# Residual adds and one weight remainder moved from VectorE to accumulating DMAs, two more block pairs, and modulation work placed elsewhere, in a two-layer hybrid DiT kernel

## The chip, the cores and the metric

The kernel runs on one core of a Trainium2 chip. The metric is the device time of one execution in microseconds (us), and the median over runs counts. TensorE is PE below, VectorE DVE, ScalarE ACT, GpSimd POOL; SyncE (SP) issues the loads.

## The reference, cut to what matters

A batch of one holds 256 latent tokens and 256 context tokens of width 1024, so 512 columns run through layer 0. Layer 0 mixes by a short convolution, layer 1 by attention; the context is dropped inside layer 1.

```python
mod  = (silu(c) @ mod_w[i] + mod_b[i]).reshape(bsz, 3, 3, 1, D_MODEL)   # shift, scale, gate of 3 branches
lat  = lat + 0.5 * mod[:, 0, 2] * _swiglu(_modulate(lat, norm_g[i, 0], mod[:, 0, 0], mod[:, 0, 1]), w13, w2)
h    = _modulate(lat, norm_g[i, 1], mod[:, 1, 0], mod[:, 1, 1])          # rms norm, scale, shift
lat  = lat + mod[:, 1, 2] * mixer(h)                                     # conv (layer 0), attention (layer 1)
lat  = lat + 0.5 * mod[:, 2, 2] * _swiglu(_modulate(lat, norm_g[i, 2], ...), w13, w2)
# the context goes through the same lines with modc, until attention has read it
def _swiglu(h, w13, w2):
    gte, up = jnp.split(h @ w13, 2, axis=-1)
    return (jax.nn.silu(gte) * up) @ w2
```

All data is float32.

## The kernel before

**Split products.** Every float32 operand of a product is split into a high part (`hi`, rounded to the PE's float32r by an ACT copy) and a low part (`lo = src - hi`, a DVE subtract); `split` (L107) does both. A product is three matmuls: hi*hi, hi*lo, lo*hi (`mm3`, L127). Weights are loaded by SP into `wr` (8 buffers of 128x1024), and split into `wh`, `wl` (4 buffers of each).

**Tokens lie along the free axis.** The residual stream `x` is 128 x 8 x 512: 8 tiles of 128 channels, 256 latent and 256 context columns. Stream `s` 0 is the latent, 1 the context. Four stages run over both streams: the first feed-forward block ("ffn(0,0)", L1060), the convolution (L1063) with its output product, ffn(0,1) and ffn(1,0). Attention and the last feed-forward block run over the latent alone.

**A feed-forward block** (`ffn`, L754) goes in three parts of 8, 7 and 7 hidden tiles ("thirds"). Of each hidden tile, gate and up are either computed as they are (`w13_mm`: 48 matmuls of 512 columns), or by `Pair` (L675), a block scheme that needs seven products of half blocks in place of eight (84 matmuls of 256 columns). `AS_IS` (L25) lists the tiles of the first third that are computed as they are. A pair needs sums of activation blocks (`sums`, tiles `T1` to `T4`) and of weight blocks (`sums`, L696: three DVE instructions on the raw weights, and splits); its block A22 is split into `w4h`, `w4l` (two buffers of each, L709) and used last, in `four`.

**The second product** (`project`, L569) turns the hidden tiles of a third into 8 output tiles, m = 0 to 7: two or three first ones together, then one by one. `finish` (L547) adds each to the residual: for both streams one DVE instruction `x = py * gate + x` that reads PSUM (L553). In the last third, and in the convolution's output product, a `tail` follows each output tile: `square_add` (L247) squares the tile on ACT and adds to `acc` on DVE. There the last two tiles, m = 6 and 7, are made separately for each stream, first the latent, so that the latent's norm (`rms_sum`: sum over channels by PE on `acc` and the last square, tile `ss`) can run under the context's matmuls. Norm, shift and splits of the next input follow. The places where such a tail runs: end of ffn(0,0), convolution's output product, end of ffn(0,1), end of ffn(1,0).

**Modulation.** The vectors `mod` of both layers are computed on DVE in 224 units in all, each a multiply-reduce over 128x1024 (`mod_unit`, L167, tile `junk`), with weights loaded by SP through the same `wr` buffers (from `in_modT`), two units or four to a 1024-wide load pair. They are strewn over the program: `tick(n)` (L210) adds to a debt and emits units. Where a consumer is reached (`mod_ready`, L217), what is missing is emitted at once. A gate is taken as a whole at the first `finish` of a block (`lazy_gate`), and halved for the feed-forward blocks by a DVE instruction (L239).

**Order.** The start (up to L1044) and the attention's heads have an order written out by hand; elsewhere a scheduler orders the instructions of each engine, and each engine then runs in order. Buffers: `gm` and `sg` (3 of each, 128x512) hold intermediate products and squares; PSUM has 6 tiles for products.

Of the kernel before, what the change touches and what calls it, by code (L numbers as in the profile page):

```python
# [9 lines left out]
F32 = mybir.dt.float32  # L10
# [11 lines left out]
NM = 22  # L22
THIRDS = (8, 7, 7)

AS_IS = {(0, 0): range(3, 8), (0, 1): (), (1, 0): ()}  # L25

EARLY = 4
HEADS = 8
# [19 lines left out]
def hybrid_kernel(ctx: ExitStack, tc: tile.TileContext, a: dict, out: bass.AP):  # L48
# [13 lines left out]
    def nm(s):  # L62
        uid[0] += 1
        return f"{s}{uid[0]}"
# [102 lines left out]
    def mod_unit(l, ch, pair, raw, j, v):  # L167

        mt = mod_tile(l, ch)
        kt = pair * 2 + j  # L170
        col = ch * KT + kt
        junk = mp.tile([P, D], BF16, name=nm("junk"), tag="junk", bufs=1)
        nc.vector.tensor_tensor_reduce(  # L173
            out=junk,
            in0=raw[j],
            in1=scbc[:, v, :],
            scale=1.0,
            scalar=modb[:, l, col : col + 1],
            op0=ALU.mult,
            op1=ALU.add,  # L180
            accum_out=mt[:, kt, v : v + 1],
        )
        done[l, ch] += 1

    def streams(l, ch):
        return 1 if l == 1 and ch >= 5 else 2
# [23 lines left out]
    def tick(n):  # L210

        owed[0] += n
        while (jobs or units) and owed[0] >= 1:
            owed[0] -= 1
            next_unit()

    def mod_ready(l, ch):  # L217
        while not ((l, ch) in done and done[l, ch] == 8 * streams(l, ch)):
            next_unit()
        return modv[l, ch]  # L220
# [10 lines left out]
        return t  # L231

    def gate_of(l, j):
        m = mod_ready(l, 3 * j + 2)
        if j == 1:
            return m
        t = const.tile([P, KT, 2], F32, name=f"G{l}{j}", tag=f"G{l}{j}")
        nv = 1 if (l, j) == (1, 2) else 2
        nc.vector.tensor_scalar(  # L239
            out=t[:, :, :nv], in0=m[:, :, :nv], scalar1=0.5, scalar2=None, op0=ALU.mult  # L240
        )
        return t


    accs = {}
# [299 lines left out]
        return tail  # L545

    def finish(m, ps, c0, c1, gate, tail, wide=False):  # L547
        g = gate()
        for s in range(2):
            for o in [s * S - c0] if not wide else range(0, T2 if s == 0 else 0, S):  # L550
                if not c0 <= s * S < c1:
                    continue
                nc.vector.scalar_tensor_tensor(  # L553
                    out=x[:, m, s * S : s * S + S],
                    in0=ps[:, o : o + S],
                    scalar=g[:, m, s : s + 1],
                    in1=x[:, m, s * S : s * S + S],
                    op0=ALU.mult,
                    op1=ALU.add,
                )  # L560
        if tail:
            tail(m, c0, c1)
# [6 lines left out]
    def project(ws, src, nk, gate, tail, tot, late, ev, between=()):  # L569

        def products(ps, w, ks, c0, c1, wide=True):
            ms = [src(k, c0, c1) for k in ks]
            if wide and len(ms[0]) == 3:
                return mm_wide(ps, [w(k) for k in ks], ms, ks[0] == 0, ks[-1] == nk - 1)
            for k, m in zip(ks, ms):  # L580
                mm3(ps[:, : c1 - c0], w(k), m[:2], k == 0, k == nk - 1)

        nf = 3 if between else 2
        ahead = {}

        def get(m):
            for i in range(m, min(m + 3, KT)):
                if i not in ahead:
                    ahead[i] = ws(i)
            return ahead[m]  # L590

        w2 = [get(m) for m in range(nf)]
        p2 = [psum("py") for _ in range(nf)]
        cut = nk - 2 if between else nk - 1
        for i in range(nf):
            products(p2[i], w2[i], range(cut), 0, tot)
            if i < len(between):
                between[i]()
        if between:
            for i in range(nf):  # L600
                products(p2[i], w2[i], (nk - 2,), 0, tot)
        for i in range(nf):
            products(p2[i], w2[i], (nk - 1,), 0, tot)
            finish(i, p2[i], 0, tot, gate, tail, len(src(0, 0, tot)) == 3)
            tick(ev)

        for m in range(nf, KT - late):
            if tail and tot == S and m == KT - 2:
                ready()
            w = get(m)  # L610
            ps = psum("py")
            wide = len(src(0, 0, tot)) == 3 and m < KT - 1
            products(ps, w, range(nk), 0, tot, wide)
            finish(m, ps, 0, tot, gate, tail, wide)
            tick(ev)
        if late:

            wl = [get(m) for m in (6, 7)]
            if tail:
                ready()  # L620
            for s in range(2):
# [53 lines left out]
    class Pair:  # L675
# [4 lines left out]


        def __init__(self, src, h):
            self.h, self.w = h, {}
# [12 lines left out]
        def sums(self, n):  # L696

            r1, r2 = self.raw
            s1, s2 = r1[:, :T2], r1[:, T2:]
            tt = nc.vector.tensor_tensor  # L700
            if n == 0:
                tt(out=s1, in0=s1, in1=r2[:, :T2], op=ALU.subtract)
                tt(out=s2, in0=s2, in1=s1, op=ALU.subtract)
                self.keep(("S1", "S2"), r1)
                return
            self.w["A22"] = [
                wp.tile([P, T2], F32R, name=nm(t), tag=t, bufs=2) for t in ("w4h", "w4l")
            ]
            split(*self.w["A22"], r2[:, :T2])  # L709
            v = lambda t: t.rearrange("p (a c) -> p a c", a=2)  # L710
            tt(  # L711
                out=v(r2), in0=v(r2), in1=s2.unsqueeze(1).to_broadcast([P, 2, T2]),
                op=ALU.subtract,
            )
            self.keep(("S3", "S4"), r2)
# [38 lines left out]
    def ffn(l, b, h, tot, gate, tail, gs=(), ev=1.5, z=None):  # L754
        gs = list(gs)
        i0 = 0
        for t, n in enumerate(THIRDS):
            between = ()
            if tot == T2:
# [22 lines left out]
                for i in range(len(gs), n):  # L782
                    if t == 0 and not heads and i in AS_IS[l, b]:
# [12 lines left out]
                        w13_mm(pp, w, h, range(4, KT), 0, T2)  # L796
                        gs.append(new_pair("g"))
                        w13_post(pp, gs[-1], 0, T2)
                        tick(4)
                        continue  # L800
                    if heads:
                        pr = heads.pop(0)
# [44 lines left out]
            def ws2(m):  # L847
# [13 lines left out]
                gate, tail if end else None, tot, 2 if end and tot == T2 else 0, ev, between,  # L861
            )
            gs = []

    def lazy_gate(l, j):
        box = []

        def get():
            if not box:
                box.append(gate_of(l, j))  # L870
            return box[0]

        return get


    h = Plain()
# [170 lines left out]
    for i in range(3):  # L1047
        gs0.append(new_pair("g"))
        w13_post(pps[i], gs0[i], 0, T2)

    with tc.issue_after(rows["last"]):
        convk = cload("convk", [P, 3, KT])
        qg = cload("qg", [P, 1])
        kg = cload("kg", [P, 1])
        cosT = cload("cosT", [P, S])
        sinT = cload("sinT", [P, S])


    hn = Plain()
    ffn(0, 0, h, T2, lazy_gate(0, 0), tail_norm(0, 1, hn), gs0, 2)  # L1060
    h = hn

    zs = []  # L1063
    for m in range(KT):
# [4 lines left out]
        for c0, c1 in ((0, S), (S, T2)) if m == 0 else ((0, T2),):  # L1069
# [14 lines left out]
        nc.vector.tensor_scalar(  # L1084
            out=d, in0=u, scalar1=convk[:, 1, m : m + 1], scalar2=None, op0=ALU.mult
        )
# [11 lines left out]
        nc.vector.tensor_tensor(out=z, in0=d, in1=pb, op=ALU.mult)  # L1098
        zs.append(new_pair("z"))
        split(zs[m][0], zs[m][1], z)  # L1100
        tick(5)

    def by_pairs(key, box=None):
        box = box or {}
# [235 lines left out]
    with tc.manual_schedule(engines={e.engine for e in (nc.tensor, nc.vector, nc.scalar, nc.gpsimd)}):  # L1340
# [29 lines left out]
    hn, hz = Beside(), Early()  # L1370
    roomy.append(True)
    project(
        by_pairs("wo", wos), lambda k, c0, c1: aos[k], KT, lazy_gate(1, 1), tail_early(1, 2, hn, hz), S, 0, 0,
    )
    ffn(
        1, 1, hn, S, lazy_gate(1, 2),
        lambda m, c0, c1: nc.sync.dma_start(out[m], x[:, m, :S]), z=hz,
    )

# [79 lines left out]
```

## Time and profile before

| what | value |
|---|---|
| runs of before | 1571.21, 1571.43 and 1567.75 us; median 1571.21 |
| profiled execution | 1571.47 us; its span from first to last instruction 1569.7 us, so 1.8 us lie around it |
| busy share: PE, DVE, ACT, POOL | 99%, 85%, 47%, 2% |
| mean granted TensorE clock | 0.998 |

A profile is read here in this order: the page's busy shares; the chain of work that ended last; then the waits of the engine that the chain names, in the stretch that a change touches. PE's durations overlap, since matmuls are pipelined: one of 512 columns is shown as 389 ns though the next one starts 227 ns later, so the pitch of starts counts, not the duration. "DMA issues" give the time from issue to landing.

### The profile page before, as it was taken

Reading aid. Unit: us, or ns where it says so; the run is one execution under the profiler, and the core shown is the slowest. Engines: PE = TensorE matmul, PEld = TensorE weight load, DVE = VectorE, ACT = ScalarE, POOL = GpSimd, SP = SyncE. Lnnn points to the kernel's source line nnn. Section 1 sums busy time; section 2 is a strip of 40 time slices with the busy share of each in tenths; the row PEclk is TensorE's granted clock in tenths of the full one; section 3 lists DMA queues with packets and bytes.
Section 4 is the critical chain, followed back from the end, with each engine's and each line's share of the span. In section 5 each row is a group of like instructions: output and inputs, shape, how many; then the busy total and the mean of one; then the engine's idle time right before and its main releaser. Section 6 shows DMA issues by size and latency. Waiting matters only on the chain.

```text
span 1569.7 us, 25671 instructions
## 1 busy us (share of the span) xinstructions
PE 1557.7 (99%) x10210; PEld 1422.0 (91%) x10210; DVE 1333.4 (85%) x2129; ACT 733.8 (47%) x1213; POOL 25.4 (2%) x20
## 2 busy tenths in 40 slices
PE   9999999999999999999999999999999999999999
PEld 7888998999888899989899899999899889898888
DVE  5998789899997698978989989969978887887676
ACT  5622452545322365435345465435345445674553
POOL 0000000000000000000000000000000002300000
PEclk9999999999999999999999999999999999999999
DMA  9675246355565323542533614533733853366562
GB/s 373 224 237 180 89 132 187 107 173 159 194 209 166 114 75 108 177 146 87 189 126 117 196 41 135 187 108 118 239 112 114 265 154 106 123 207 221 171 199 75
DMA packets 72120, 248.80 MB, mean 159 GB/s; under 512 B 9024, under 2 KB 10816, under 8 KB 72000
## 3 DMA queue, kind: packets, MB, share of 16 engines
q1 hardware_dynamic: 69408, 245.40, 48.0%
q10 hardware_dynamic: 2592, 1.76, 0.4%
q8 instruction: 80, 1.31, 0.3%
q14 instruction: 40, 0.33, 0.1%
HBM read 244.77 MB, written 1.05 MB: 157 GB/s over the span
## 4 chain that ended last, share of the span: by engine, by line
PE 88%; DVE 6%; DMA 2%; ACT 2%; issue 1%; POOL 0%; POOLq 0%; SPq 0%; ACTq 0%; DVEq 0%
PE py L131 8%; PE py L132 8%; PE py L133 8%; PE p L131 6%; PE p L133 6%; PE p L132 6%; PE q L133 5%; PE q L131 4%; PE q L132 4%; PE py L139 2%; PE pu L139 2%; PE pg L139 2%; PE pg L132 1%; PE pg L133 1%; DMA wr<-in_w 1%; PE pu L132 1%
## 5 line engine op out<-in xcount | busy, mean ns | idle before, releaser
L108 ACT ACTIVATE wh<-wr 128x1024 fp32r<-128x1024 f32 (+2 forms) x442 | 393.7, 916 | 361.9 <-PE py L132 119.6
L109 DVE TENSOR_TENSOR wl<-wr,wh 128x1024 fp32r<-128x1024 f32 (+2 forms) x442 | 454.5, 1048 | 95.1 <-ACT wh L108 76.2
L173 DVE CUSTOM_DVE_ANT_0 junk<-wr,scbc,modb 128x1024 bf16<-128x1024 f32 x218 | 279.4, 1282 | 15.2 <-DMA wr<-in_modT 13.1
L131 PE MATMUL py<-gh,wh 128*128 128x512 f32 (+1 forms) x570 | 214.7, 377 | 0.0
L132 PE MATMUL py<-gl,wh 128*128 128x512 f32 (+1 forms) x570 | 214.0, 375 | 0.0
L133 PE MATMUL py<-gh,wl 128*128 128x512 f32 (+1 forms) x570 | 213.9, 375 | 0.0
L133 PEld LDWEIGHTS py<-gh,wl 128*128 128x128 f32 x570 | 108.3, 190 | 19.0
L131 PEld LDWEIGHTS py<-gh,wh 128*128 128x128 f32 x570 | 108.5, 190 | 18.4
L132 PEld LDWEIGHTS py<-gl,wh 128*128 128x128 f32 x570 | 108.5, 190 | 18.2
L131 PE MATMUL p<-th,wh 128*128 128x256 f32 x432 | 122.3, 283 | 0.0
L132 PE MATMUL p<-tl,wh 128*128 128x256 f32 x432 | 122.3, 283 | 0.0
L133 PE MATMUL p<-th,wl 128*128 128x256 f32 x432 | 122.2, 283 | 0.0
L553 DVE SCALAR_TENSOR_TENSOR x<-py,G,x 128x256 f32<-128x256 f32 x189 | 83.5, 479 | 36.3 <-PE py L133 25.1
L133 PE MATMUL q<-bh,wl 128*128 128x256 f32 x320 | 91.5, 286 | 0.1
L131 PE MATMUL q<-bh,wh 128*128 128x256 f32 x320 | 90.9, 284 | 0.4 <-ACT wh L108 0.4
L132 PE MATMUL q<-bl,wh 128*128 128x256 f32 x320 | 90.5, 283 | 0.0
L132 PEld LDWEIGHTS p<-tl,wh 128*128 128x128 f32 x432 | 82.8, 192 | 0.3
L131 PEld LDWEIGHTS p<-th,wh 128*128 128x128 f32 x432 | 82.8, 192 | 0.3
L133 PEld LDWEIGHTS p<-th,wl 128*128 128x128 f32 x432 | 82.8, 192 | 0.0
L108 ACT ACTIVATE w4h<-wr 128x512 fp32r<-128x512 f32 x54 | 33.8, 625 | 75.1 <-DMA wr<-in_w 56.9
L108 ACT ACTIVATE gh<-gm 128x512 fp32r<-128x512 f32 x66 | 41.6, 630 | 56.0 <-DVE gm L751 53.8
L711 DVE TENSOR_TENSOR wr<-wr,wr 128x1024 f32<-128x1024 f32 x54 | 66.0, 1222 | 0.7
(303 smaller groups left out, 3946.3 us busy)
## 6 DMA issues: line engine op xcount, KB each, us to landing
wr<-in_w SPq DMA_DIRECT2D x176, 512.0 KB, 4.5
wr<-in_modT SPq DMA_DIRECT2D x122, 512.0 KB, 4.5
wr<-in_w2b SPq DMA_DIRECT2D x64, 448.0 KB, 3.9
wr<-in_w2a SPq DMA_DIRECT2D x32, 512.0 KB, 4.7
pm<-in_mod SPq DMA_DIRECT2D x16, 512.0 KB, 10.2
wr<-in_cw_cx SPq DMA_DIRECT2D x16, 512.0 KB, 4.7
wr<-in_cw_b SPq DMA_DIRECT2D x8, 512.0 KB, 4.4
wr<-in_cw_out SPq DMA_DIRECT2D x8, 512.0 KB, 3.9
```

Source lines behind the costliest of these rows:

```text
L108: nc.scalar.activation(out=hi, in_=src, func=AF.Copy)
L109: return nc.vector.tensor_tensor(out=lo, in0=src, in1=hi.bitcast(F32), op=ALU.subtract)
L131: nc.tensor.matmul(ps, wh, mh, start=first, stop=False, **kw)
L132: nc.tensor.matmul(ps, wh, ml, start=False, stop=False, **kw)
L133: nc.tensor.matmul(ps, wl, mh, start=False, stop=last, **kw)
L139: nc.tensor.matmul(ps, w[0], m[2], start=first and n == 0, stop=False)
L173: nc.vector.tensor_tensor_reduce(out=junk, in0=raw[j], in1=scbc[:, v, :], scale=1.0, scalar=modb[:, l, col : col + 1], op0=ALU.mult, op1=A ...
L553: nc.vector.scalar_tensor_tensor(out=x[:, m, s * S : s * S + S], in0=ps[:, o : o + S], scalar=g[:, m, s : s + 1], in1=x[:, m, s * S : s * ...
L711: tt(out=v(r2), in0=v(r2), in1=s2.unsqueeze(1).to_broadcast([P, 2, T2]), op=ALU.subtract,)
```

## The change

- `finish`: for both streams together (columns 0 to 511), and outside a tail or for m below 4 in a tail, ACT writes `gy = py * gate` (two instructions of 256 columns) to a `gm` or `sg` buffer, and a POOL DMA adds `gy` to `x`. In a tail the square of these tiles then waits for that DMA. The other tiles stay with DVE.
- `Pair.sums`: ACT writes `w4h`, then `w4l = -w4h`; a POOL DMA adds the raw block from HBM to `w4l`. The DVE subtract goes.
- `AS_IS` of ffn(0,0) shrinks from tiles 3 to 7 to tiles 3 to 5: tiles 6 and 7 become pairs.
- The factor 0.5 goes into the modulation units (and two small DVE instructions halve the bias); a gate is waited for two tiles at a time.
- `project` emits no modulation after m = 5 where two late tiles follow, and none after m = 6 and 7 elsewhere; the other counts rise (for example from 1.5 to 2.6 and 1.6 in ffn(1,0)). In `w13`'s as-is tiles 3 in place of 4 units, in the convolution 4 in place of 5.
- One multiply in the convolution (`d`) moves from DVE to ACT.

```diff
-AS_IS = {(0, 0): range(3, 8), (0, 1): (), (1, 0): ()}
+AS_IS = {(0, 0): range(3, 6), (0, 1): (), (1, 0): ()}
...
-            scale=1.0,
+            scale=0.5 if ch in (2, 8) else 1.0,
...
     def gate_of(l, j):
...
+        ch = 3 * j + 2
+        def get(m):
+            while done.get((l, ch), 0) < (m // 2 + 1) * 2 * streams(l, ch):
+                next_unit()
+            return modv[l, ch]
+        return get
...
     def finish(m, ps, c0, c1, gate, tail, wide=False):
-        g = gate()
+        g = gate(m)
+        if c1 - c0 == T2 and (not tail or m < 4):
+            t = tp.tile([P, T2], F32, name=nm("gy"), tag="sg" if m % 2 else "gm", bufs=3)
+            for s in range(2):
+                d = slice(s * S, s * S + S)
+                nc.scalar.activation(
+                    out=t[:, d], in_=ps[:, d], func=AF.Copy, scale=g[:, m, s : s + 1]
+                )
+            nc.gpsimd.dma_start(out=x[:, m, :], in_=t, accum_op=ALU.add)
+            if tail:
+                tail(m, c0, c1)
+            return
...
             finish(m, ps, 0, tot, gate, tail, wide)
-            tick(ev)
+            if m < (5 if late else 6):
+                tick(ev)
...
-            split(*self.w["A22"], r2[:, :T2])
+            w4h, w4l = self.w["A22"]
+            nc.scalar.activation(out=w4h, in_=r2[:, :T2], func=AF.Copy)
+            nc.scalar.activation(out=w4l, in_=w4h.bitcast(F32), func=AF.Copy, scale=-1.0)
+            nc.gpsimd.dma_start(out=w4l, in_=self.src[:, 1024 : 1024 + T2], accum_op=ALU.add)
...
-                        tick(4)
+                        tick(3)
...
+    for ch in (2, 8):
+        b = modb[:, :, ch * KT : ch * KT + KT]
+        nc.vector.tensor_scalar(out=b, in0=b, scalar1=0.5, scalar2=None, op0=ALU.mult)
...
-    ffn(0, 0, h, T2, lazy_gate(0, 0), tail_norm(0, 1, hn), gs0, 2)
+    ffn(0, 0, h, T2, gate_of(0, 0), tail_norm(0, 1, hn), gs0, (3, 3))
...
-        nc.vector.tensor_scalar(
-            out=d, in0=u, scalar1=convk[:, 1, m : m + 1], scalar2=None, op0=ALU.mult
-        )
+        nc.scalar.activation(out=d, in_=u, func=AF.Copy, scale=convk[:, 1, m : m + 1])
...
-        tick(5)
+        tick(4)
...
-        lazy_gate(0, 1), tail_norm(0, 2, hn), T2, 2, 1.5,
+        gate_of(0, 1), tail_norm(0, 2, hn), T2, 2, 2,
...
-    ffn(0, 1, h, T2, lazy_gate(0, 2), tail_norm(1, 0, hn), (), 1.7)
+    ffn(0, 1, h, T2, gate_of(0, 2), tail_norm(1, 0, hn), (), (2.8, 2.4))
...
-    ffn(1, 0, h, T2, lazy_gate(1, 0), tail_norm(1, 1, hn), (), 1.5)
+    ffn(1, 0, h, T2, gate_of(1, 0), tail_norm(1, 1, hn), (), (2.6, 1.6))
```

More of the change, by code (lines that the diff above doesn't have):

```diff
@@ L233, in gate_of @@
     def gate_of(l, j):
[L234 to L238, printed above, removed]
-        nc.vector.tensor_scalar(
-            out=t[:, :, :nv], in0=m[:, :, :nv], scalar1=0.5, scalar2=None, op0=ALU.mult
-        )
-        return t
+        ch = 3 * j + 2
[4 more added lines that the diff above has]
+        return get
     accs = {}
@@ L682, in __init__ @@
         def __init__(self, src, h):
-            self.h, self.w = h, {}
+            self.h, self.w, self.src = h, {}, src
             self.raw = [load_raw(src[:, c : c + 1024]) for c in (0, 1024)]
@@ L752, in four, with ffn @@
             split(g[0], g[1], self.gm)
-    def ffn(l, b, h, tot, gate, tail, gs=(), ev=1.5, z=None):
+    def ffn(l, b, h, tot, gate, tail, gs=(), ev=(0, 0), z=None):
         gs = list(gs)
@@ L860, in ffn @@
                 else lambda k, c0, c1: (cur[k][0][:, c0:c1], cur[k][1][:, c0:c1]), n,
-                gate, tail if end else None, tot, 2 if end and tot == T2 else 0, ev, between,
+                gate, tail if end else None, tot, 2 if end and tot == T2 else 0, ev[end], between,
             )
             gs = []
[L865 to L873, printed above, removed]
     h = Plain()
@@ L1083, in hybrid_kernel @@
         d = tp.tile([P, T2], F32, name=nm("d"), tag="gm", bufs=3)
-        nc.vector.tensor_scalar(
-            out=d, in0=u, scalar1=convk[:, 1, m : m + 1], scalar2=None, op0=ALU.mult
-        )
+        nc.scalar.activation(out=d, in_=u, func=AF.Copy, scale=convk[:, 1, m : m + 1])
         u2 = u.rearrange("p (s t) -> p s t", s=2)
@@ L1372, in hybrid_kernel @@
     project(
-        by_pairs("wo", wos), lambda k, c0, c1: aos[k], KT, lazy_gate(1, 1), tail_early(1, 2, hn, hz), S, 0, 0,
+        by_pairs("wo", wos), lambda k, c0, c1: aos[k], KT, gate_of(1, 1), tail_early(1, 2, hn, hz), S, 0, 0,
     )
     ffn(
-        1, 1, hn, S, lazy_gate(1, 2),
+        1, 1, hn, S, gate_of(1, 2),
         lambda m, c0, c1: nc.sync.dma_start(out[m], x[:, m, :S]), z=hz,
```

## Prediction

> **What bounds the kernel now.** The page first.
>
> ```profile
> span 1569.7 us, 25671 instructions
> ...
> PE 1557.7 (99%) x10210; PEld 1422.0 (91%) x10210; DVE 1333.4 (85%) x2129; ACT 733.8 (47%) x1213; POOL 25.4 (2%) x20
> ...
> PE 88%; DVE 6%; DMA 2%; ACT 2%; issue 1%; POOL 0%; POOLq 0%; SPq 0%; ACTq 0%; DVEq 0%
> ```
>
> PE is busy 99%, and the chain of waits is PE for 88%. So taking work from DVE shortens nothing by itself; it counts only where PE waits for DVE. The waits of PE between 45 and 1300 us, where all edits lie:
>
> ```profile
> PE ss L268 <- DVE acc L259: 1.5, 1, 1.5
> PE pg L132 <- DVE bl L109: 1.3, 2, 1.0
> PE pq L131 <- ACT hh L305: 0.4, 1, 0.4
> PE q L131 <- ACT wh L108: 0.4, 1, 0.4
> PE pq L132 <- DVE hl L306: 0.3, 1, 0.3
> ```
>
> The longest is the norm at the end of ffn(1,0). Its timeline (start, duration, engine, instruction):
>
> ```profile
> 1248.92 1.28 DVE L173 CUSTOM_DVE_ANT_0 junk<-wr,scbc,modb 128x1024 bf16<-128x1024 f32 x1
> 1250.24 1.28 DVE L173 CUSTOM_DVE_ANT_0 junk<-wr,scbc,modb 128x1024 bf16<-128x1024 f32 x1
> 1251.45 0.88 DVE L553 SCALAR_TENSOR_TENSOR x<-py,G,x 128x256 f32<-128x256 f32 x2
> 1252.24 1.22 DVE L109 TENSOR_TENSOR wl<-wr,wh 128x1024 fp32r<-128x1024 f32 x1
> 1253.37 0.76 DVE L259 TENSOR_TENSOR acc<-acc,sq 128x256 f32<-128x256 f32 x2
> 1254.04 0.48 DVE L553 SCALAR_TENSOR_TENSOR x<-py,G,x 128x256 f32<-128x256 f32 x1
> 1256.91 1.28 DVE L173 CUSTOM_DVE_ANT_0 junk<-wr,scbc,modb 128x1024 bf16<-128x1024 f32 x1 [2.39 <-DMA wr<-in_modT]
> 1258.13 0.42 DVE L259 TENSOR_TENSOR acc<-acc,sq 128x256 f32<-128x256 f32 x1
> ...
> 1251.56 2.25 SPq L104 DMA_DIRECT2D wr<-in_modT  x2
> ...
> 1256.80 0.28 PE L133 MATMUL py<-gh,wl 128*128 128x256 f32 x1
> 1258.60 0.38 PE L268 MATMUL ss<-ones,acc 128*128 128x1 f32 x2 [1.52 <-DVE acc L259]
> ```
>
> DVE stands behind a modulation unit whose weights were issued at 1251.56 and used at 1256.91, and `acc` behind that. PE loses 1258.60 - 1256.80 less a pitch of 0.12 = 1.68 us. The windows over the stall and after it show a second loss (PE, PEld, DVE, ACT, POOL busy; PEclk; DMA share; GB/s):
>
> ```profile
> 1252.00:1259.00 7.00, 5.47 (x46) 5.27 (x45) 4.61 (x10) 2.54 (x4) 0.00 (x0) 1.00 0.62 218
> 1259.60:1266.40 6.80, 6.80 (x34) 6.80 (x33) 4.31 (x13) 2.93 (x6) 0.00 (x0) 0.50 0.50 146
> ...
> 575.63 0.39 PE L132 MATMUL pg<-bl,wh 128*128 128x256 f32 x1 [1.01 <-DVE bl L109]
> ```
>
> For 6.8 us the granted clock is 0.50: half of it, 3.4 us, is lost. Over the span this is 3.4/1569.7 = 0.2%, just what a mean clock of 0.998 lacks. The 1.0 us wait at 575.63 brought no such stretch (the mean leaves room for one). So a stall of 1.7 us cost 5.1 us, one of 1.0 us only itself.
>
> **The change part by part.**
>
> ```profile
> 646.54 0.39 PE L131 MATMUL py<-gh,wh 128*128 128x512 f32 x1
> ...
> 648.80 0.39 PE L132 MATMUL py<-gl,wh 128*128 128x512 f32 x1
> ...
> 649.37 0.28 PE L132 MATMUL p<-tl,wh 128*128 128x256 f32 x1
> ...
> 650.57 0.28 PE L133 MATMUL p<-th,wl 128*128 128x256 f32 x1
> ```
>
> Two more pairs. Ten pitches lie between the first two rows, 0.226 us each, ten between the last two, 0.120 each. Two as-is tiles are 2 x 48 x 0.226 = 21.7 us, two pairs 2 x 84 x 0.120 = 20.2: -1.5 us. A pair costs DVE more, about 3.3 us by the rows below (1024 columns 1222 ns, 512 columns 687 ns; a net 2 x 1024 and 2 x 512 more, less A22), while the as-is tiles' units fall from 20 to 9 (11 x 1.36 = 15 us less). The cover is that room; without it the pairs' splits would be late.
>
> ```profile
> L553 DVE SCALAR_TENSOR_TENSOR x<-py,G,x 128x256 f32<-128x256 f32 x189 | 83.5, 479 | 36.3 <-PE py L133 25.1
> L711 DVE TENSOR_TENSOR wr<-wr,wr 128x1024 f32<-128x1024 f32 x54 | 66.0, 1222 | 0.7
> ...
> L109 DVE TENSOR_TENSOR w4l<-wr,w4h 128x512 fp32r<-128x512 f32 x54 | 37.1, 687 | 1.2 <-ACT w4h L108 1.0
> L257 DVE COPY acc<-sq 128x256 f32<-128x256 f32 x11 | 2.7, 286 | 0.0
> ...
> L108 ACT ACTIVATE w4h<-wr 128x512 fp32r<-128x512 f32 x54 | 33.8, 625 | 75.1 <-DMA wr<-in_w 56.9
> L734 ACT COPY gm<-q 128x256 f32<-128x256 f32 x54 | 19.7, 365 | 41.2 <-PE q L133 41.2
> ...
> POOL pn L1297 <- DVE r L1294: 1323.8, 4, 1320.7
> ```
>
> Residuals by DMA: 64 tiles (3 x 20, and 4 in the convolution's output product) take 128 x 479 ns = 61 us off DVE and put 128 x 365 = 47 on ACT. A22: 54 subtracts, 37 us, off DVE; 56 more copies of 625 ns, 35 us, on ACT. POOL gets 120 DMAs; it has nothing else to do until 1320 us (last row). ACT stays near 52% and hides its part. What DVE's room is worth is only PE's waits for splits at the pairs' starts; the largest, with two more at the queries' start:
>
> ```profile
> 943.29 0.39 PE L131 MATMUL q<-bh,wh 128*128 128x256 f32 x1 [0.39 <-ACT wh L108]
> ...
> 1270.90 0.38 PE L131 MATMUL pq<-hh,wh 128*128 128x256 f32 x1 [0.43 <-ACT hh L305]
> 1271.54 0.39 PE L132 MATMUL pq<-hl,wh 128*128 128x256 f32 x1 [0.26 <-DVE hl L306]
> ```
>
> In pitches (a wait shows as idle only beyond the overlap) the splits' waits add up to 2.8 us; bounds 0 and 2.8, I take half, -1.4. For the queries the built order of after lets two query products take turns over each arriving `hh`, `hl`, where before one ran alone: bounds 0 and 1.5, taken -1.1. The `bl` wait hangs on the norm after PE's own sum and stays. Gates by pairs of tiles, the halving and `d` on ACT: nothing, beside DVE's room; if that were gone, under 1 us.
>
> Modulation off the last tiles. In after one unit, not two, stands ahead of m = 5 in ffn(1,0), so the load at 1251.56 starts 1.3 us earlier. The unit then ends 1.4 us earlier, and 1.68 shrinks to about 0.3, too short for the half clock: -1.4 - 3.4 = -4.8. Bounds: 0 (the load comes as late as before) and -5.1.
>
> The new wait. In a tail the squares of m = 0 to 3 wait for the adds, in ACT's order: adds 0 and 1, squares 0 and 1, gates of m = 2 and 3, squares 2 and 3. Behind them on DVE wait `acc` and all it does for m = 4 and 5. Call the landing L. In ffn(1,0)'s times: m = 5 ends at 1250.8, each of m = 2 to 5 takes 21 x 0.226 = 4.8 us, so m = 1 ends at 1235.8; its gate copy ends at 1236.9, square 1 at 1237.5 + L, the copies of m = 2 and 3 at 1239.1 + L, square 3 at 1239.7 + 2L, `acc` at 1240.5 + 2L. After it DVE has for m = 4: 0.88 + 1.22 + 0.76 + one unit 1.36; for m = 5: 0.88 + 1.22 + 0.76; then `x` 0.4, unit 1.36, `x` 0.4 and the last square 0.4: 9.6 to 10.0 us until the sum, wanted at 1256.9. So DVE must begin by 1246.9: L up to 3.2 us is free, and each us beyond costs 2. By the built orders the tails of ffn(0,1) and the convolution have no units there (free to 4.2), and ffn(0,0) has its sum nine matmuls later (free to 3.7).
>
> ```profile
> wr<-in_w SPq DMA_DIRECT2D x176, 512.0 KB, 4.5
> ...
> wr<-in_w2b SPq DMA_DIRECT2D x64, 448.0 KB, 3.9
> ...
> rt<-kn ACTq DMA_DIRECT2D x16, 64.0 KB, 2.7
> out_lat<-x SPq DMA_DIRECT2D x8, 128.0 KB, 1.7
> ```
>
> No row has an accumulating or a POOL-issued DMA. An add moves 256 KB and touches it twice, so the rows bound L by 1.7 (half the bytes, quiet) and 4.5 (twice the bytes, among other loads). I take 3.1, the middle: no cost. For small new waits I add 0.8, an estimate of half the remaining splits' waits. [...] `w4l` has two buffers and is used a pair later, some 10 us (84 x 0.120): any L in the bounds is hidden.
>
> Sum, against the profiled 1571.5: -1.5 - 1.4 - 1.1 - 4.8 + 0.8 = -8.0: 1563.5. The median shown is 0.3 lower, so the same within a rounding.
>
> **The rivals.** Late adds (slower). At L = 4.8 the four tails cost 2 x (1.6 + 1.1 + 0.6 + 0.6) = 7.8, and those over 1.5 us, two, bring a half clock each: 6.8. 1563.5 + 14.6 = 1578. It decides from about L = 4.7 (beyond 0.3% of 1571, 4.7 us, which a measurement of this kernel can tell from no change). For it: the tail's DMA share of 0.62 above. Against: the 448 KB row lands in 3.9 in such stretches.
>
> The late load stays: the adds share the DMA engines with `in_modT`, and the unit holds up the sum as before. Then -4.8 falls away: 1568.3, within the bound.
>
> POOL held off. Each add is preceded by POOL's work on it; if DVE's instructions shut POOL out while they run, L grows by a unit's 1.3 us to 4.4: tails 2 x (1.2 + 0.7 + 0.2 + 0.2) = 4.6 and two half clocks 6.8, 1575. [...]
>
> **How the numbers follow.** Forecast 0.58, its own range 1560 to 1567 (all gains full: -1.5 - 2.8 - 1.5 - 5.1 = 1560.6); of it 0.54 are faster by over 0.3% and 0.04 not. Late adds 0.26, all slower. Late load 0.09, same. POOL held off 0.07: 0.04 same, 0.03 slower. Faster 0.54, same 0.17, slower 0.29. The range 1560 to 1579 holds the first, third and fourth and half of the late adds.
>
> **What would show it.** Right: mean clock 1.000 before the end of ffn(1,0) and no 0.50 window there; `x <- gy` landing in 2 to 4 us; no wait of `ss` over 1 us; 84 matmuls of 256 in place of 48 of 512 for two tiles; POOL idle in between. Wrong: ACT's `sq` waiting for the adds over 4 us and DVE's `acc` behind it, new half-clock windows at the four tails, `junk` still waiting for `in_modT` at the last sum, or PE waiting for `w4l`.

## The result and the profile after

The changed kernel takes 1660.34 us (median of 4 runs, 1653.94 to 1663.69), the kernel before 1571.32: ratio 1.0565, interval 1.0527 to 1.0604. It is 89 us slower where 8 us less were forecast, and far outside the range. The profiled execution is the fastest of the four, 1653.94 us. From the page of the changed kernel (the line PEclk is the granted clock in 40 slices, in tenths; q0 is the queue of the DMAs that POOL issues, with packets, MB and share of 16 engines' span; the last rows are DMA issues, KB each, us to landing):

```profile
span 1652.1 us, 26266 instructions
...
PE 1577.1 (95%) x10282; PEld 1443.2 (87%) x10282; DVE 1262.2 (76%) x1951; ACT 820.4 (50%) x1417; POOL 130.5 (8%) x140
...
PEclk9999999997999989999999989999989989999999
...
q1 hardware_dynamic: 69408, 245.40, 45.1%
q0 software_dynamic: 17280, 31.46, 11.1%
...
wr<-in_w SPq DMA_DIRECT2D x176, 512.0 KB, 4.8
...
x<-gy POOLq DMA_DIRECT2D x64, 256.0 KB, 6.9
w4l<-in_w POOLq DMA_DIRECT2D x56, 256.0 KB, 5.9
```

DVE did get its room: 85% became 76%. But PE fell from 99% to 95%, and the clock from 0.998 to 0.975. The adds land after 6.9 us, where the forecast took 3.1 and bounded it by 4.5. Where PE waits, in the view of its waits (us in total, times, longest):

```profile
PE q L131 <- ACT gm L751: 30.3, 7, 8.0
PE ss L268 <- DVE acc L259: 28.1, 5, 10.6
PE ss L268 <- ACT sq L251: 5.0, 3, 4.4
```

Two places, then. `ss` is the norm at the end of a tail, the place of the rival "late adds". `q <- gm` is the start of a third, where the first pairs after a second product wait; no rival had it. Together 63.4 us. The span grew by 82.4; the rest is mostly the clock. The clock's records of both traces hold no rate but 1.0 and 0.5, so a mean of 0.975 comes to 0.025 x 1652.1 / 0.5 = 83 us at half clock, against 6 before. By the trace's clock records some 30 us of them lie inside the waits themselves, so about 25 us are lost beside the waits.

**A start of a third** (ffn(1,0), the costliest). The windows of the changed kernel over the second product before it and over the stall (PE, PEld, DVE, ACT, POOL busy; PEclk; DMA share; GB/s):

```profile
1192.00:1214.00 22.00, 22.00 (x99) 18.22 (x98) 14.35 (x20) 10.79 (x21) 6.16 (x7) 1.00 1.04 307
1223.40:1233.70 10.30, 4.44 (x21) 4.44 (x22) 7.42 (x9) 3.21 (x5) 0.00 (x0) 0.50 0.58 187
```

The DMA engines are full (1.04) for 22 us. The kernel before runs the same second product 64 us earlier, and there the share is 0.62:

```profile
1130.00:1150.00 20.00, 20.00 (x90) 16.57 (x89) 18.86 (x31) 4.75 (x6) 0.00 (x0) 1.00 0.62 213
```

Over the six second products outside the tails the share is 0.80 to 1.03 in the changed kernel and 0.46 to 0.69 before, so this one is the fullest. The issues of the 9 us from 1193, in the DMA view of that window of the changed kernel:

```profile
q1 hardware_dynamic: 499, 1.83, 65.0%
q0 software_dynamic: 317, 0.59, 36.0%
...
wr<-in_w SPq DMA_DIRECT2D x8, 512.0 KB, 10.8
x<-gy POOLq DMA_DIRECT2D x4, 256.0 KB, 8.7
```

Eight weight loads land after 10.8 us in the median; over the whole program it is 4.8. These eight hold all 8 buffers of the `wr` ring. So SP waits 12.7 us for a free one, and the next two loads, of `in_modT`, are issued only at 1214.85 and 1221.37; they land at an ordinary pace, 5.2 and 3.8 us later. The end of this delay in the timeline of DVE, ACT and PE (start, duration, instruction, idle before):

```profile
1220.05 1.28 DVE L173 CUSTOM_DVE_ANT_0 junk<-wr,scbc,modb 128x1024 bf16<-128x1024 f32 x1 [4.63 <-DMA wr<-in_modT]
...
1225.27 1.28 DVE L173 CUSTOM_DVE_ANT_0 junk<-wr,scbc,modb 128x1024 bf16<-128x1024 f32 x1 [2.19 <-DMA wr<-in_modT]
...
1227.09 0.68 DVE L716 TENSOR_TENSOR wr<-wr 128x512 f32<-128x512 f32 x1
...
1227.89 1.06 ACT L108 ACTIVATE wh<-wr 128x1024 fp32r<-128x1024 f32 x1 [10.29 <-DVE wr L716]
1228.85 0.35 ACT L751 COPY gm<-q 128x256 f32<-128x256 f32 x1
...
1229.26 0.58 PE L131 MATMUL q<-bh,wh 128*128 128x256 f32 x1 [8.03 <-ACT gm L751]
```

Read it from below: PE waits 8 us for a copy of 0.35 us. The copy stands on ACT behind a weight split, the split waits 10.3 us for DVE's sums of weight blocks (L716), and DVE, in order, stands before them at the two modulation units whose loads were issued late.

**A tail** (end of ffn(1,0)). POOL's issues, ACT's squares, the last unit on DVE and the sum on PE:

```profile
1311.13 1.79 POOL L557 DMA_DIRECT2D x<-gy  x2 [23.92 <-ACT gy L554]
...
1316.99 0.63 ACT L251 ACTIVATE sq<-x 128x512 f32<-128x512 f32 x1 [3.86 <-DMA x<-gy]
1320.22 0.64 ACT L251 ACTIVATE sq<-x 128x512 f32<-128x512 f32 x1 [2.59 <-DMA x<-gy]
...
1338.87 1.28 DVE L173 CUSTOM_DVE_ANT_0 junk<-wr,scbc,modb 128x1024 bf16<-128x1024 f32 x1 [1.71 <-DMA wr<-in_modT]
...
1340.56 0.59 PE L268 MATMUL ss<-ones,acc 128*128 128x1 f32 x2 [9.58 <-DVE acc L259]
```

The adds of m = 0 and 1 are issued together and land one behind the other: square 0 can start 5.9 us after the first issue, square 1 after 9.1. Then the gates of m = 2 and 3 follow, and the same again. And a `junk` unit still waits for `in_modT` right before the last `acc`, as in before.

### The profile page after: what moved, and what is told of

Its sections match the earlier page's. It is cut to its first block, busy times and chain, and to the rows that moved or that the text cites. A ratio compares the mean times of both kernels' runs of the same rounds, so it can differ in the third digit from the quotient of the medians.

```text
span 1652.1 us, 26266 instructions
## 1 busy us (share of the span) xinstructions
PE 1577.1 (95%) x10282; PEld 1443.2 (87%) x10282; DVE 1262.2 (76%) x1951; ACT 820.4 (50%) x1417; POOL 130.5 (8%) x140
## 3 DMA queue, kind: packets, MB, share of 16 engines
q1 hardware_dynamic: 69408, 245.40, 45.1%
## 5 line engine op out<-in xcount | busy, mean ns | idle before, releaser
L173 DVE CUSTOM_DVE_ANT_0 junk<-wr,scbc,modb 128x1024 bf16<-128x1024 f32 x222 | 284.5, 1281 | 39.1 <-DMA wr<-in_modT 36.8
L131 PE MATMUL p<-th,wh 128*128 128x256 f32 x448 | 126.8, 283 | 0.0
L132 PE MATMUL p<-tl,wh 128*128 128x256 f32 x448 | 126.8, 283 | 0.0
L133 PE MATMUL p<-th,wl 128*128 128x256 f32 x448 | 126.7, 283 | 0.0
L726 POOL DMA_DIRECT2D w4l<-in_w x56 | 49.0, 874 | 729.5 <-ACT w4l L725 654.1
L715 DVE TENSOR_TENSOR wr<-wr,wr 128x512 f32<-128x512 f32 x56 | 38.6, 690 | 77.9 <-DMA wr<-in_w 77.6
L557 POOL DMA_DIRECT2D x<-gy x64 | 56.2, 932 | 488.7 <-ACT gy L554 465.1
L758 ACT ACTIVATE sg<-sg 128x512 f32<-128x512 f32 x56 | 35.4, 632 | 101.3 <-DVE sg L757 101.3
## 6 DMA issues: line engine op xcount, KB each, us to landing
pm<-in_mod SPq DMA_DIRECT2D x16, 512.0 KB, 10.2
```

Source lines behind the costliest of these rows:

```text
L131: nc.tensor.matmul(ps, wh, mh, start=first, stop=False, **kw)
L132: nc.tensor.matmul(ps, wh, ml, start=False, stop=False, **kw)
L133: nc.tensor.matmul(ps, wl, mh, start=False, stop=last, **kw)
L173: nc.vector.tensor_tensor_reduce(out=junk, in0=raw[j], in1=scbc[:, v, :], scale=0.5 if ch in (2, 8) else 1.0, scalar=modb[:, l, col : col ...
L557: nc.gpsimd.dma_start(out=x[:, m, :], in_=t, accum_op=ALU.add)
L726: nc.gpsimd.dma_start(out=w4l, in_=self.src[:, 1024 : 1024 + T2], accum_op=ALU.add)
```

## The experiments

First the four ways to take the DMAs back; all start from the changed kernel, and each was compared with the kernel before, 1570.05 us in this group.

**No accumulating DMA at all.** `finish` and `sums` as before, the rest as changed.

```diff
-        if c1 - c0 == T2 and (not tail or m < 4):
+        if False:
...
-            nc.scalar.activation(out=w4l, in_=w4h.bitcast(F32), func=AF.Copy, scale=-1.0)
-            nc.gpsimd.dma_start(out=w4l, in_=self.src[:, 1024 : 1024 + T2], accum_op=ALU.add)
+            split(*self.w["A22"], r2[:, :T2])
```

> The changed kernel with every accumulating DMA taken back: DVE adds all residuals again and subtracts A22's low part; the two more pairs, the gates by pairs of tiles, the modulation placement and `d` on ACT stay. Theory DMA (the 120 accumulating DMAs cause the whole loss, by the waits in the tails and by late weight loads at the starts of the thirds): about 1563 us, the forecast's other terms, mean clock near 1.000, no stall of PE over 2 us between 45 and 1300 us. Theory PLACEMENT (gates, modulation and DVE's order cause a good part): above 1590 us, with the stalls at the thirds' starts (ACT's copy of gm behind a weight split) still 4 us or more each.

Measured 1578.4 us, ratio 1.0051 (1.0033 to 1.0070): between the two expectations. So 82 of the 89 us come with the DMAs and the ACT copies that feed them, and of the `q <- gm` waits 0.5 us is left. But the other edits cost 8 us where the forecast had them gain, and at the end of ffn(1,0) `ss` still waits, 2.6 us at the longest:

```profile
PE ss L268 <- DVE acc L259: 3.1, 3, 2.6
PE q L131 <- ACT wh L108: 1.8, 4, 0.9
```

**Only the DMAs into `w4l`.** The first of the two edits above alone.

> The changed kernel with the 64 residual adds back on DVE; the 56 DMAs into w4l stay. If the residual adds alone cause the loss: as without any accumulating DMA, about 1563 us. If all accumulating DMAs slow the weight loads by the DMA time they take (56 of 120): about half of the 48 us of the thirds' starts stays, about 1590 us, and loads of in_w land in more than 5.2 us on the mean.

Measured 1573.55 us, ratio 1.0014 (0.9998 to 1.0031): 4.8 less than without any DMA, and again between the two expectations. Alone, with no residual adds beside them, these 56 DMAs do no harm here.

**Only the residual adds.** The second edit alone.

> The changed kernel with A22's low part back on DVE (no DMAs into w4l); the 64 residual adds stay. If the residual adds alone cause the loss: 1645 to 1660 us. If the DMAs into w4l carry half of the late loads: about 1625 to 1635 us, with shorter stalls at the thirds' starts and residual adds that land earlier than the 6.9 us of the changed kernel.

Measured 1641.92 us, ratio 1.0454 (1.0431 to 1.0477). Neither expectation held: the DMAs into `w4l` cost 18.4 us in the changed kernel, where the residual adds run too. The second ACT copy of each pair comes and goes with them and was not tried by itself.

**No adds in the tails.**

```diff
-        if c1 - c0 == T2 and (not tail or m < 4):
+        if c1 - c0 == T2 and not tail:
```

> The changed kernel with residual adds by DMA only outside the tails (48 of 64 stay, and the DMAs into w4l): in the tails DVE adds. The stalls at the four norms with the half-clock stretches that follow come to about 59 us in the changed kernel, those at the starts of the thirds to about 48. If the two are separate causes: about 1595 to 1605 us, norm stalls below 2 us each, thirds' starts as before. If the tails' waits cause both: below 1575 us.

Measured 1620.71 us, ratio 1.0317 (1.0287 to 1.0348). The norms are free of it, the starts of the thirds are not: two separate causes, the thirds' dearer by 20 us than was expected.

Next, why weight loads are late outside the tails (before: 1568.9 in this group). All three have no other accumulating DMA than the one named.

**Adds of zeros.** DVE adds as before; then, outside the tails, POOL adds a tile of zeros to the same `x`, and nobody waits for it until the next block.

```diff
+        if c1 - c0 == T2 and not tail:
+            nc.gpsimd.dma_start(out=x[:, m, :], in_=spare[0], accum_op=ALU.add)
```

> The kernel without accumulating DMAs (1578.4 us) plus, outside the tails, one DMA per residual tile that adds a tile of zeros to x after DVE's own add: 48 DMAs of 256 KB that nobody waits for, no copy on ACT, no gm or sg buffer held. Theory SHARED ENGINES (the adds take DMA time from the weight loads, so the pairs at the starts of the thirds wait for their weights): 1600 to 1625 us, with stalls of 2 to 6 us where PE waits for ACT's copy of gm behind a weight split, and loads of in_w with a mean of 5.4 us or more. Theory HELD BUFFERS (gm and sg stay taken until an add lands) or ACT LATE (the copies delay ACT's splits): 1575 to 1583 us, no such stall.

**Plain copies at the same places.**

```diff
+        if c1 - c0 == T2 and not tail:
+            nc.gpsimd.dma_start(out=spare[0], in_=x[:, m, :])
```

> The same with plain DMAs: at the same 48 places x is copied to a spare tile, nothing is added. If the accumulation itself makes the transfer dear: packets of 2 KB at about half of the 188 ns of the changed kernel's adds, landing near 3 us, and less than half of the loss that the adds of zeros bring. If the bytes and their small packets alone count: the same packet time, landing and loss as with the adds of zeros.

Measured 1590.88 us (ratio 1.0134, 1.0112 to 1.0156) with zeros added, and 1580.23 (1.0072, 1.0054 to 1.0090) with copies, against 1578.4 without either. The adds lie between the expectations, under the 1600 to 1625 of shared engines, and the copies land after 4.5 us, not 3. But the adds cost 12.5 us and the copies 1.8, which is no more than can be told from nothing, and the stalls stand at the same places as in the changed kernel, though shorter, without a wait of PE for any add. PE's waits with adds of zeros:

```profile
PE q L131 <- ACT gm L754: 7.8, 4, 3.9
PE p L131 <- ACT sg L748: 2.2, 1, 2.2
```

The DMA parts of the two pages, first the adds of zeros:

```profile
q0 software_dynamic: 6912, 12.59, 4.7%
...
x<-spare POOLq DMA_DIRECT2D x48, 256.0 KB, 6.9
```

and the copies:

```profile
q0 software_dynamic: 3840, 12.59, 2.0%
...
spare<-x POOLq DMA_DIRECT2D x48, 256.0 KB, 4.5
```

The same 12.59 MB. An add takes 0.047 x 1585.1 / 48 = 1.55 us of all 16 engines, a copy 0.020 x 1578.6 / 48 = 0.66. A weight load of twice the bytes takes, by q1's 45.1% for 245.40 MB in 1652.1 us, 3.04 us per MB, so 1.6. An add of 256 KB thus occupies the engines as long as a whole weight load of 512 KB. The traces show the add in packets of 2 KB and the copy in packets of 4 KB; whether the adding or the smaller packets make it dear was not tried.

**ACT's copies without the DMA.** ACT writes `gy`, DVE adds it to `x`.

```diff
-            nc.gpsimd.dma_start(out=x[:, m, :], in_=t, accum_op=ALU.add)
+            nc.vector.tensor_tensor(out=x[:, m, :], in0=t, in1=x[:, m, :], op=ALU.add)
```

> The changed kernel with ACT's scaled copies, but DVE adds each copy to x where the DMA did; A22's low part is DVE's too, so no accumulating DMA is left. Theory ACT LATE: above 1595 us, stalls at the starts of the thirds as in the changed kernel. Theory SHARED ENGINES and waits in the tails: 1575 to 1585 us, like the kernel without accumulating DMAs (1578.4), no stall over 3 us.

Measured 1586.67 us, ratio 1.0108 (1.0093 to 1.0123): between the two expectations. Its waits for `gm` are a third of the 20.5 us with the residual adds by DMA:

```profile
PE q L131 <- ACT gm L747: 6.7, 3, 2.9
PE ss L268 <- DVE acc L259: 2.8, 2, 2.0
```

So ACT's copies, with an add by DVE, carry a part of their own, 8 us. The scheduler also orders ACT and DVE otherwise around them; which of the two it is was not taken apart.

The third group parts the small edits (before: 1569.57).

**The placement alone.** No accumulating DMA, and the as-is tiles of before.

```diff
-AS_IS = {(0, 0): range(3, 6), (0, 1): (), (1, 0): ()}
+AS_IS = {(0, 0): range(3, 8), (0, 1): (), (1, 0): ()}
```

> The kernel before plus the changed modulation placement, the gates by pairs of tiles, the halving in the units and `d` on ACT; no accumulating DMA, and the as-is tiles 3 to 7 as before. The kernel without accumulating DMAs lost 8 us against before. If the two more pairs lose them (DVE has no room for their 6.6 us): 1566 to 1571 us here. If the placement loses them: 1576 to 1581 us here. By the forecast's term for the modulation (-4.8) it would be 1565 us, with no wait of PE's ss for acc over 1 us at the end of ffn(1,0); the kernel without accumulating DMAs still showed one of 2.8 us there, so this is doubted.

Measured 1574.52 us, ratio 1.0032 (1.0021 to 1.0043): 5 us slower, neither of the expected ranges; `ss` waits 2.2 us at the end of ffn(1,0), more than before's 1.5. At the queries' start the two waits of before are still there:

```profile
PE pq L131 <- ACT hh L305: 0.4, 1, 0.4
PE pq L132 <- DVE hl L306: 0.3, 1, 0.3
```

From the first to the last matmul of the queries it is 41.52 us here, without any DMA, and before alike.

**Two more pairs alone**, on the kernel before.

```diff
-AS_IS = {(0, 0): range(3, 8), (0, 1): (), (1, 0): ()}
+AS_IS = {(0, 0): range(3, 6), (0, 1): (), (1, 0): ()}
```

> The kernel before with tiles 6 and 7 of ffn(0,0) as pairs, nothing else. If pairs without room on DVE are late: 1573 to 1579 us, with new waits of PE for weight splits between 60 and 170 us. If they bring what their matmuls save: 1568 to 1570 us (-1.5).

Measured 1570.74 us, ratio 1.0011 (1.0001 to 1.0021). The 1.5 us of the matmuls do not show in the median, and the measured time lies between the two expected ranges. In the trace, the first third of ffn(0,0) from the end of its hand-written start to the last matmul of its second product takes 97.15 us in place of 97.69: a saving of 0.5, beside a new wait `q <- gm` of 0.7 us. Where the rest of the time goes was not found.

**Adds outside the tails alone**, with A22's low part on DVE.

> The changed kernel with residual adds by DMA outside the tails alone; A22's low part is DVE's. The adds of zeros at the same places cost 12.5 us, the copies on ACT about 8 (with those in the tails). If these two make up the loss outside the tails: 1595 to 1602 us. If the adds and the DMAs into w4l are dear only together: the same, and the 1620.7 of the kernel without tail adds stands over 18 us above it. If holding gm and sg until the landing counts too: 1605 us or more here.

Measured 1605.06 us, ratio 1.0223 (1.0203 to 1.0243): 26.7 above the kernel without DMAs. The 1605 us that would tell for the held buffers are just met, so a run had to decide it (below).

**The DMAs into `w4l` on the kernel before.**

```diff
+            nc.scalar.activation(out=w4h, in_=r2[:, :T2], func=AF.Copy)
+            nc.scalar.activation(out=w4l, in_=w4h.bitcast(F32), func=AF.Copy, scale=-1.0)
+            nc.gpsimd.dma_start(out=w4l, in_=self.src[:, 1024 : 1024 + T2], accum_op=ALU.add)
```

> The kernel before with only A22's low part made by DMA from ACT's copy (54 DMAs). On the changed kernel without residual adds these DMAs went with 4.8 us less (1573.6 against 1578.4). If that is DVE's room for the pairs' splits, here too: 1564 to 1568 us. If it was worth something only with two more pairs: 1569 to 1573 us.

Measured 1574.58 us, ratio 1.0026 (1.0014 to 1.0038): 5 us slower. The gain of 4.8 seen above does not carry over. Several of PE's waits are longer here (`ss` for `acc` 2.3 us in place of 1.5, new ones for `gh` and `gl` of 0.8 and 0.6); what causes them was not taken apart.

The last group was made for what was still open (before: 1570.28).

**Adds in the tails alone**, A22's low part on DVE.

```diff
-        if c1 - c0 == T2 and (not tail or m < 4):
+        if c1 - c0 == T2 and tail and m < 4:
```

> The changed kernel with residual adds by DMA in the tails alone (16), A22's low part on DVE, no adds outside. The kernel without accumulating DMAs takes 1578.4. By the forecast's arithmetic with landings near 5 to 8 us (two adds one behind the other): stalls of 3 to 9 us at each of the four norms and half-clock stretches of 3 to 14 us behind each, 1605 to 1625 us. If the tails are hit only because the adds outside them, or the DMAs into w4l, make the DMA engines busy: landings of 3 to 4 us and 1580 to 1590 us.

Measured 1616.43 us, ratio 1.0290 (1.0271 to 1.0309): 38.0 above the kernel without DMAs, and 26.7 + 38.0 = 64.7 is about the 63.5 of both together. PE is idle for 47.1 us of the profiled span, against 18.2 without DMAs; the remaining 8 us of the longer span are the clock's. The end of ffn(1,0) on ACT, and POOL's issues, in this kernel's timeline:

```profile
1272.24 1.55 ACT L554 ACTIVATE gy<-py,mod 128x256 f32<-128x256 f32 x4
...
1279.27 0.63 ACT L251 ACTIVATE sq<-x 128x512 f32<-128x512 f32 x1 [3.80 <-DMA x<-gy]
1282.75 0.63 ACT L251 ACTIVATE sq<-x 128x512 f32<-128x512 f32 x1 [2.84 <-DMA x<-gy]
1283.28 1.55 ACT L554 ACTIVATE gy<-py,mod 128x256 f32<-128x256 f32 x4
...
1287.95 0.63 ACT L251 ACTIVATE sq<-x 128x512 f32<-128x512 f32 x1 [2.27 <-DMA x<-gy]
1291.44 0.63 ACT L251 ACTIVATE sq<-x 128x512 f32<-128x512 f32 x1 [2.86 <-DMA x<-gy]
...
1273.46 1.76 POOL L557 DMA_DIRECT2D x<-gy  x2 [350.99 <-DVE wl L109]
1284.51 1.76 POOL L557 DMA_DIRECT2D x<-gy  x2 [9.29 <-DVE acc L259]
```

The forecast's order, just as it was drawn. From the end of the copies to the second square: 1282.75 - (1272.24 + 1.55) = 9.0 us, then 1291.44 - (1283.28 + 1.55) = 6.6. The forecast had 2L free up to 6.4; 15.6 - 6.4 = 9.2 us of wait follow. PE's waits:

```profile
PE ss L268 <- DVE acc L259: 26.9, 4, 9.7
PE ss L268 <- ACT sq L251: 4.4, 3, 3.7
```

9.7 is the one of ffn(1,0). The arithmetic holds; the landing was wrong. The 16 adds of this kernel land after 3.3 to 10.2 us, 5.9 in the median. The first add of the second pair (issued at 1284.51) meets no load and lands in 3.3 us, near the forecast's 3.1; the one issued right behind it lands 3.5 us later. The first pair meets weight loads on its way, and its adds land after 5.7 and 8.5 us.

**Adds of zeros and ACT's copies together**, outside the tails: ACT writes `gy`, DVE adds it, then the DMA adds zeros. `gm` and `sg` are free as soon as DVE has read them.

```diff
-            nc.gpsimd.dma_start(out=x[:, m, :], in_=t, accum_op=ALU.add)
...
+            nc.vector.tensor_tensor(out=x[:, m, :], in0=t, in1=x[:, m, :], op=ALU.add)
+            nc.gpsimd.dma_start(out=x[:, m, :], in_=spare[0], accum_op=ALU.add)
+            return
```

> Outside the tails: ACT's scaled copy, added to x by DVE, and then a DMA that adds zeros to x; nobody waits for it and gm and sg come free with DVE's add. No other accumulating DMA. If late weight loads and ACT's copies make up the loss of the adds outside the tails (1605.1) together: 1597 to 1608 us. If the held buffers carry a part: 1590 to 1597 us, and the stalls at the starts of the thirds are shorter than the up to 6.1 us of the kernel with adds outside the tails.

Measured 1603.65 us, ratio 1.0204 (1.0182 to 1.0227), as much as with the real adds (1605.06); its longest `q <- gm` wait is 7.4 us. So held buffers are not needed for the loss, though DVE has 48 adds here that the real adds spare it. Late loads and ACT's copies together give 25 of the 27 us of the adds outside the tails, where singly they cost 12.5 and 8 (the 8 with the tails' copies): together more than their sum.

**The modulation units behind the sum.** One edit on the kernel before: the units of attention's first three ticks may not start on DVE before the last `acc` add of the latent.

```diff
-                    nc.vector.tensor_tensor(out=accs[s], in0=accs[s], in1=part, op=ALU.add)
+                    accs["add", s] = nc.vector.tensor_tensor(
+                        out=accs[s], in0=accs[s], in1=part, op=ALU.add
+                    ).ins
...
-    tick(1)
+    with tc.issue_after(accs["add", 0]):
+        tick(1)
```

> The kernel before with one edit: the modulation units that attention's first three ticks emit are held behind the last acc add of the latent at the end of ffn(1,0). In the built order of before and of the changed kernel these units stand ahead of that add, whatever the project's own ticks do. If they are what the norm waits for: the 1.7 us wait of ss and the half-clock stretch after it (3.4 us) go, 1563 to 1567 us. If the add is late by itself: 1568 to 1571 us, the wait stays. If the units then delay the queries' splits instead: 1566 to 1572 us with longer waits for hh, hl or wl after the norm.

Measured 1566.78 us, ratio 0.9978 (0.9970 to 0.9987): 0.22% faster than before, and the only kernel of this study that beats both. Its timeline at the end of ffn(1,0), DVE and then PE:

```profile
1255.34 0.43 DVE L259 TENSOR_TENSOR acc<-acc,sq 128x256 f32<-128x256 f32 x1 [0.55 <-ACT sq L251]
1255.68 1.28 DVE L173 CUSTOM_DVE_ANT_0 junk<-wr,scbc,modb 128x1024 bf16<-128x1024 f32 x1
...
1257.55 0.28 PE L270 MATMUL ss<-ones,acc 128*128 128x1 f32 x2
```

The add stands ahead of the unit now; `ss` comes without a wait, and the clock stays full behind it (windows of the same kernel):

```profile
1250.00:1257.00 7.00, 7.00 (x55) 6.73 (x54) 4.82 (x10) 3.60 (x5) 0.00 (x0) 1.00 0.47 149
1257.00:1264.00 7.00, 7.00 (x61) 7.00 (x61) 5.46 (x14) 4.39 (x9) 0.00 (x0) 1.00 0.51 153
```

61 matmuls in 7 us (the norm's small ones among them), where before did 34 in 6.8 after its stall. That stretch is not in every execution of before: of the 15 of this group, three had a mean clock of 1.000 and took 1567.08 to 1567.96 us, the other twelve 0.996 to 0.999 and 1569.05 to 1574.51. So the gain of 3.5 us in the median is mostly the clock's.

## Why the prediction was wrong, step by step

- **The landing of an add, the step that failed first.** The forecast took the landing L as 3.1 us ("the middle: no cost") and bounded it by 4.5. Measured: 6.9 in the median, and 5.9 with the tails' adds alone. For an add that stands alone 3.1 was nearly right: such a one lands in 3.3 us. But the adds do not stand alone. The tails issue two at a time, which land one behind the other, 1.4 to 4.7 us apart in the kernel with the tails' adds alone, and the second square waits for both. And weight loads are under way at the same time, which the upper bound allowed for by the median of loads. That an add touches its bytes twice was the author's assumption in the bounds, and no run shows it. An add also costs the DMA engines 2.4 times what a copy of the same bytes does (1.55 against 0.66 us). No term was for a queue.
- **The tails' arithmetic** was right: order of ACT's work, two landings in a row, 6.4 us free, and each us beyond on PE. It gave 9.2 us where 9.7 was measured. The rival "late adds" named this mechanism and had 14.6 us for L = 4.8; at 9.0 and 6.6 us the tails alone cost 38. So the mechanism was foreseen, and its price missed by the landing.
- **What the adds take from others** was the second failed step, and a whole missing case. The late-load rival let the adds share the engines with `in_modT` at one place. That they crowd the engines in every second product (a share of 0.80 to 1.03), so that the next third's weights come late, was in no term: 26.7 us for these adds with ACT's copies, 42.3 together with the DMAs into `w4l` (1620.71 less 1578.4). ACT's copies were put at nothing too ("ACT stays near 52% and hides its part"): ACT's share came as forecast, 50%, and still the copies with an add by DVE cost 8 us.
- **`w4l`, "any L in the bounds is hidden".** True of its own landing: it takes 4.2 to 8.9 us, beyond the bound, and still PE never waits for `w4l`. But these 56 DMAs, with their ACT copies, add 18.4 us to the kernel with residual adds. That the crowded engines are the reason is likely but not shown by a run of its own; the adds of zeros show that a DMA that nobody waits for has a price there (12.5 us for 48).
- **DVE's room for splits (-1.4).** DVE's share fell by 9 points, and the splits at the thirds' starts came later than ever. Room on DVE was not what they waited for once the loads were late. No kernel here shows the gain of 1.4.
- **Modulation off the last tiles (-4.8).** The gain was real, its cause was misplaced. The units ahead of the last `acc` are not those of the product's own ticks: they belong to attention's ticks, and the scheduler moves them up. On the kernel before this is shown: held back by one edit, stall and half clock go, 3.5 us of the 4.8. In the changed kernel they stand ahead of the add too, the changed counts did not touch them, and `ss` waits 2.6 us without any DMA; the edit was not tried on it.
- **Two more pairs (-1.5), gates and placement (nothing).** The pairs alone bring 1.2 us more, not less, a difference at the edge of what can be told; the placement alone costs 5. What of the placement costs it was not taken apart. The queries' -1.1 is nothing: without DMAs their two waits and their 41.52 us stay as before.
- **POOL held off by DVE.** No run isolates it, but the traces speak against it. In the kernel with adds in the tails alone, one add is issued at 370.73, while a modulation unit runs on DVE (370.42 to 371.70), and lands in 3.35 us; the one at 1284.51, issued while DVE is idle, in 3.34. In the changed kernel POOL's instructions for the 64 adds take 0.86 to 1.22 us, 0.87 in the median, so the longest is 0.36 us above the shortest, where the rival had 1.3.
- **The chances.** 0.29 was given to slower, and the range ended at 1579 because the bound of L did. The bound came from transfers of another kind.
- **Slips in the sums that decide nothing.** By its rows a pair costs DVE 3.1 us more, not 3.3. In this tail m = 2 is made together with m = 0 and 1, so only m = 3 to 5 take 4.8 us each; the 1235.8 is right. By its own prices the late adds reach 1575.7 us, where they decide, at L = 4.5 and not 4.7. The rival "POOL held off" counts two half clocks at L = 4.4, where by its own bound of 1.5 us only one wait is long enough, which gives 1571.5 us.

In sum, from the runs: 8 us for placement and pairs, 38 for the tails' waits with the half clock behind them, 27 for late loads and ACT's copies outside the tails, 18 for the DMAs into `w4l` beside the adds: 91, against 89 measured. The steps are differences of whole kernels, and some of them depend on each other.

## What to carry to other kernels

An accumulating DMA takes a vector engine's work to the DMA engines, so cost it there first: its time on all engines, beside the share that the loads already use in that very stretch (here 1.55 us for 256 KB, where the loads had a share of 0.62 before), and then its landing as one of a queue (here 6.9 us in the median, against 3.3 for one that stood alone). A kernel that lives from a ring of weight buffers can feel a late load in the next stage, on another engine (here PE's wait of 8.0 us): look for it at the next place where fresh weights are needed. And before an instruction in front of a critical one is blamed on the code beside it, look in the built order for where it was written; a scheduler may have brought it from far.

## What the runs showed of the hardware that was not expected

- An add of 256 KB takes as much engine time as a load of 512 KB, 1.55 against 1.6 us, and a plain copy of 256 KB takes 0.66. The queue's packets differ too: 6912 for the adds of zeros, 3840 for the copies of the same bytes.
- Loads and adds had even shares of the engines where both had work: from 1199 to 1203 in the changed kernel 224 packets of the loads' queue take 54.2% and 212 of the adds' take 53.4%, though the loads' packets carry 4 KB and the adds' 2 KB. (In the 9 us shown it is 65.0% and 36.0%, since the adds' queue is empty at first.) SP's loads got no precedence there: the eight of these 9 us land after 10.8 us in the median.
- The clock's half-rate stretch around the stall of 8 us lasts 10.2 us, and begins while PE still waits: the window from 1223.40 to 1233.70 stands at 0.50, and the wait ended at 1229.26. Of the stretch only what lies behind the stall costs. By its clock records the ten such stretches of the changed kernel last 3.41 us (three of them), 6.83 (two), 10.24 (four) and 17.07 (one). Before's wait of 1.52 us was followed by 6.8 us at 0.50. The length of a wait alone does not decide here: with the adds outside the tails alone, waits of 2.04 and 2.16 us brought no such stretch. Cut into pieces of 3.41 us, the shortest stretch, that begin where the stretches do, the traces of this study show more (15 profiles, from 45 to 1350 us): all 37 pieces at full rate with PE idle for 60% or more were followed by half rate, 6 of 10 with 50 to 60%, and 8 of 73 with 20 to 50%.
